# Per-sample sums over partitions in cross-attention: the shares as the stationary operand in four column groups, and a transpose behind them

## The chip, the cores and the metric

The kernel runs on one core of one Trainium2 chip. The metric is the device time of one execution in microseconds (us), the median over runs. Three runs of the kernel before took 1271.40, 1271.95 and 1270.92 us.

## The reference: what is computed

One inference step of a two-layer trunk runs for a prompt of 256 rows and for 8 samples of one row each; both share all weights (model width 1024). Each layer is a half SwiGLU, a mixer (a short convolution in layer 0, a gated recurrence in layer 1), a cross-attention on a memory, and a second half SwiGLU. The part touched here is the samples' cross-attention:

```python
def cross_attn(x, mk, mv, w_q, w_o):
    B, T, D = x.shape
    q = (x @ w_q).reshape(B, T, X_HEADS, X_HEAD_DIM)
    s = jnp.einsum('bthd,bnhd->bhtn', q, mk.astype(q.dtype)).astype(jnp.float32) / math.sqrt(X_HEAD_DIM)
    p = jax.nn.softmax(s, axis=-1).astype(x.dtype)
    o = jnp.einsum('bhtn,bnhd->bthd', p, mv.astype(x.dtype)).reshape(B, T, D)
    return o @ w_o
```

Each of the 8 samples has its own cached keys and values: 256 memory rows, 4 heads of 256 numbers. The prompt projects its own memory with `w_xkv`.

## The kernel before

Activations lie transposed, model width on partitions: eight blocks of 128 partitions by 264 columns (256 prompt columns, then 8 sample columns). Every projection is made three times over split numbers: a value is cut into a high part that the fast matmul format holds exactly and a low rest, and `mm3` (lines 350 to 352) multiplies high by high, high by low and low by high. Weights come as "halves" of 128x1024 through a queue of six raw buffers: SP loads them (L101), ACT rounds them to `wh` (L112), DVE or POOL subtracts to get `wl` (L127). `wh` and `wl` have five buffers each.

TensorE is kept busy by these projections. All else is cut into small generators, and the projection loops call `flow.tick()` after every few matmuls; a tick moves each of three lanes on by one step. A scheduler then sets the final order on each engine, by the program's order and by priorities (`tc.high_priority(offset=HURRY)` lifts a piece). Each engine runs its list strictly in that order.

Cross-attention (`attention`, once per layer) runs in this order: the queries of four heads (`project`), then for each head the prompt's keys and values (`do_kv`, tiles `kv`), then the output projection (`project_late`, tiles `pj` from `oh` and `ol`). In lane 1 run the prompt's scores (`psc`), softmax (`Pp`), transposes (`ppt`, then `PTh` on ACT and `PTl` on DVE) and values (`po`). In lane 0 run the samples' scores and then `sample_rest`.

In `sample_rest` the 2048 memory rows of the 8 samples lie on 128 partitions with 16 rows each (16 partitions belong to one sample). For each of two pairs of heads, DVE adds 16 value rows, weighted by their exponentials, into `acc` (a PSUM bank; L1194 and L1197) and writes the last one into `total` (128 partitions x 2 heads x 256). Every second row ends a step, and two more steps (`LAG`) follow. Then the sum over a sample's 16 partitions is taken by TensorE: `oz` (128x8) holds for a head each partition's share in its sample's column, 0 elsewhere. Line 1214 makes four matmuls per pair, with a 128x128 block of `total` stationary and `oz` moving, so that the result `spt` comes out with width on partitions, 8 columns a block. ACT rounds it into `oh` (L1221), and DVE writes the rest into `ol` (L1222), at the sample columns of this pair's four blocks.

The output projection reads those columns: `until(0)` ahead of its first blocks, and `until(1)` ahead of block 4, which is the second pair's first. So `pj` matmuls on block 4 wait for the second pair's `oh`.

Of the kernel before, what the change touches and what calls it, by code (L numbers as in the profile page):

```python
# [9 lines left out]
F32 = mybir.dt.float32  # L10
# [3 lines left out]
ALU = mybir.AluOpType  # L14
# [3 lines left out]
P = 128  # L18
# [3 lines left out]
NB = 8  # L22
# [5 lines left out]
XD = 256  # L28
RH = 8
NI = NMEM * NB // P  # L30
# [14 lines left out]
STEPS = (3, 5, 7, 9, 11, 13)  # L45
# [210 lines left out]
def trunk_step(ctx: ExitStack, tc: tile.TileContext, ins, consts, outs, stop=None):  # L256
    nc = tc.nc
# [11 lines left out]
    def aux_bank(name):  # L269
        return paux.tile([P, 512], F32, tag="aux", name=name)  # L270

    W = Weights(nc, wp)
    flow = Flow(W)
    ring = Ring(cp)

    ident = cp.tile([P, P], F32, name="ident")
# [31 lines left out]
    def order(ins, first, reason):  # L308
        info = mybir.DependencyInfo(mybir.DependencyClass.NoSync, mybir.DependencyReason.DATA)
        tc.add_manual_dep(ins.ins, first.name, info, reason=reason)  # L310
# [14 lines left out]
    def act(dst, src, func, **kw):  # L325
        in_line(nc.scalar.activation(dst, src, func, **kw))  # L326
# [647 lines left out]
    def attention(l, norm, nxt):  # L974
        with tc.tile_pool(name="at", bufs=1) as ap:
# [4 lines left out]
            for hf, tag in enumerate("hl"):  # L980
                t = ap.tile([P, KT, NC], F32, tag="o" + tag, name=f"spare{hf}", bufs=1)
# [6 lines left out]
            sc = ap.tile([P, XH, NI], F32, name="sc")  # L988
            oz = ap.tile([P, XH, NB], F32, name="oz")
            sampled, ahead = set(), []  # L990
            mx, zs, rz = (ap.tile([P, XH], F32, name=n) for n in ("mxs", "zss", "rzs"))
            tops = ap.tile([P, P], F32, name="tops")
            nc.gpsimd.memset(tops, 0.0)

            def mem_split():
                for _ in range(6):
                    yield
                W.lo = ("p",)
                for k in range(KT):
                    g = gcol("norm_mem", l, k)  # L1000
                    mg = ap.tile([P, NMEM], F32, tag="mg", name=f"mg{k}", bufs=2)
                    W.behind("s", nc.scalar.activation(mg, memT[:, k], AF.Copy, scale=g))
                    nc.scalar.copy(mh[:, k], mg)
                    nc.gpsimd.tensor_sub(ml[:, k], mg, mh[:, k].bitcast(F32))
                    yield
# [144 lines left out]
            def combine():  # L1150

                pt = aux_bank("pst")
                order(nc.tensor.transpose(pt[:XH, :P], mx, ident), flow.passed, "products in line")
                yield
                top, f, g = pt[:XH, 2 * P : 2 * P + NB], pt[:, P + 2 * XH : P + 3 * XH], pt[:, P + 3 * XH : P + 4 * XH]
                nc.vector.tensor_reduce(top, pt[:XH, :P].rearrange("h (b g) -> h b g", b=NB), axis=AX.X, op=ALU.min)
                nc.vector.tensor_copy(tops[:XH].rearrange("h (b g) -> h b g", b=NB), spread(top))
                yield
                order(
                    nc.tensor.matmul(pt[:, P : P + XH], tops, ident[:, :XH], start=True, stop=True),  # L1160
                    flow.passed,
                    "products in line",
                )
# [12 lines left out]
                nc.vector.tensor_mul(g, rz, f)  # L1176
                nc.vector.tensor_mul(
                    oz, g.unsqueeze(2).broadcast_to([P, XH, NB]), own.unsqueeze(1).broadcast_to([P, XH, NB])
                )

            def sample_rest():

                for _ in range(SLACK):
                    yield
                steps = combine()
                for pair in range(XH // 2):
                    acc = aux_bank("acc")
                    total = ap.tile([P, 2, XD], F32, tag="total", name="total", bufs=1)
                    for i in range(NI):
                        t = ring.tiles[l, "v", pair, i // 4].rearrange("p (i h d) -> p i h d", i=4, h=2)  # L1190
                        for j in range(2):
                            p, sums = sc[:, 2 * pair + j, i : i + 1], acc[:, j * XD : j * XD + XD]
                            if i == 0:
                                nc.vector.tensor_scalar(sums, t[:, i % 4, j], p, None, op0=ALU.mult)  # L1194
                            else:
                                dst = total[:, j] if i == NI - 1 else sums
                                nc.vector.scalar_tensor_tensor(  # L1197
                                    dst, t[:, i % 4, j], p, sums, op0=ALU.mult, op1=ALU.add
                                )
                        if i % 4 == 3:  # L1200
                            ring.done((l, "v", pair, i // 4))
                        if pair == 0 and i in STEPS:
                            next(steps, None)
                        if i % 2:
                            yield
                    for _ in range(LAG):
                        yield
                    pt = aux_bank("spt")
                    for j in range(2):
                        for dt in range(2):  # L1210
                            o = pt[:, (2 * j + dt) * NB : (2 * j + dt) * NB + NB]
                            d = slice(dt * P, dt * P + P)
                            order(
                                nc.tensor.matmul(o, total[:, j, d], oz[:, 2 * pair + j], start=True, stop=True),
                                flow.passed,
                                "products in line",
                            )
                    with tc.high_priority(offset=HURRY):
                        ptv = pt[:, : 4 * NB].rearrange("p (t b) -> p t b", b=NB)
                        ohv, olv = (both[tag][:, 4 * pair : 4 * pair + 4, T:] for tag in "hl")  # L1220
                        nc.scalar.copy(ohv, ptv)  # L1221
                        W.after["v"] = nc.vector.tensor_sub(olv, ptv, ohv.bitcast(F32)).ins  # L1222
                    sampled.add(pair)
                    yield

            def until(pair):
                while pair not in sampled:
# [557 lines left out]
```

## Time and profile before

The profiled execution took 1272.46 us; its span, from first to last instruction, is 1270.6 us, so 1.9 us lie around the span. The mean granted TensorE clock is 0.998 of full speed.

| what | value |
|---|---|
| median of three runs | 1271.4 us |
| profiled execution, its span | 1272.46 us, 1270.6 us |
| busy: PE, weight load, DVE, ACT, POOL | 99%, 97%, 66%, 55%, 27% |
| `spt` matmuls (L1214) | 32 records, 3.9 us busy in all |
| pair 1 in layer 0: last row of `total`, first `spt`, first `pj` that needs `oh` | 392.05, 394.60, 395.90 us |

Times in the text are microseconds from the start of the span. A group row gives line, engine, operation, output and inputs, the count, the busy time in us and the mean in ns. A timeline row gives the start, the duration, the engine, the line, the operation, and in brackets the engine's idle time before it with what ended it. One fp32 matmul leaves two records in the trace; matmuls are pipelined, so the distance between starts tells what one costs, and the duration does not.

### The profile page before, as it was taken

What the parts mean: (1) busy time and instruction counts of PE and PEld (TensorE: products, weight loads), DVE (VectorE), ACT (ScalarE), POOL (GpSimd) and SP (SyncE); (2) the same over time, 40 slices, a digit from 0 to 9 for tenths busy, and PEclk for the clock granted to TensorE, in tenths of its full rate; (3) what the DMA queues carried; (4) which work ended last, traced back from release to release, by engine and by line L of the source; (5) the groups of instructions that cost most, each with busy time, mean ns of one, the idle gap of its engine ahead of it and who ended that gap; (6) DMA issues with size and microseconds to landing.
All of it is one profiled execution on the core that took longest, in us unless ns stands there. A gap on an engine that the chain in (4) does not pass through costs nothing.

```text
span 1270.6 us, 25550 instructions
## 1 busy us (share of the span) xinstructions
PE 1257.1 (99%) x10046; PEld 1230.5 (97%) x10046; DVE 841.1 (66%) x1629; ACT 704.4 (55%) x1172; POOL 346.5 (27%) x276
## 2 busy tenths in 40 slices
PE   8999999999999999999999999999999999999997
PEld 8999999999889999999999999999999899999997
DVE  7655467768787655556655535887888787766454
ACT  6455445446665655534645544656576657766543
POOL 2211231223974211132111132000016862112220
PEclk9999999999999999999999999999999999999999
DMA  8795556656999666556666556653638997997551
GB/s 276 246 302 179 166 178 191 195 168 218 313 374 305 184 187 178 180 162 198 190 181 184 173 170 190 190 176 123 192 120 283 352 370 225 286 321 234 166 167 35
DMA packets 269899, 270.97 MB, mean 213 GB/s; under 512 B 8777, under 2 KB 259721, under 8 KB 269266
## 3 DMA queue, kind: packets, MB, share of 16 engines
q1 hardware_dynamic: 264158, 264.50, 66.8%
q10 hardware_dynamic: 5620, 4.83, 1.1%
q8 instruction: 79, 1.29, 0.4%
q14 instruction: 42, 0.34, 0.1%
HBM read 259.19 MB, written 10.10 MB: 212 GB/s over the span
## 4 chain that ended last, share of the span: by engine, by line
PE 90%; DVE 4%; DMA 2%; ACT 2%; issue 1%; POOL 0%; SPq 0%; DVEq 0%; POOLq 0%; ACTq 0%
PE pj L350 20%; PE pj L351 20%; PE pj L352 20%; PE dn L350 7%; PE dn L352 7%; PE dn L351 7%; DMA raw<-in_w_xkv_dram 2%; PE kv L1024 1%; PE kv L1026 1%; PE kv L1025 1%; DVE wl L127 1%; PE pl L1374 1%; DVE xl L376 1%; PE psc L1109 1%; ACT wh L112 1%
## 5 line engine op out<-in xcount | busy, mean ns | idle before, releaser
L127 DVE TENSOR_TENSOR wl<-raw,wh 128x1024 fp32r<-128x1024 f32 (+1 forms) x334 | 411.9, 1238 | 235.6 <-ACT wh L112 223.4
L350 PE MATMUL pj<-xh,wh 128*128 128x264 f32 x1952 | 558.0, 286 | 0.5 <-DVE g L850 0.5
L351 PE MATMUL pj<-xl,wh 128*128 128x264 f32 x1952 | 553.3, 283 | 0.0
L352 PE MATMUL pj<-xh,wl 128*128 128x264 f32 x1952 | 553.1, 283 | 0.0
L112 ACT CAST wh<-raw 128x1024 fp32r<-128x1024 f32 (+1 forms) x406 | 415.4, 1032 | 213.6 <-PE pj L351 114.4
L350 PEld LDWEIGHTS pj<-xh,wh 128*128 128x128 f32 x1952 | 367.6, 188 | 2.3 <-issue 1.4
L351 PEld LDWEIGHTS pj<-xl,wh 128*128 128x128 f32 x1952 | 368.0, 189 | 0.2
L352 PEld LDWEIGHTS pj<-xh,wl 128*128 128x128 f32 x1952 | 366.2, 188 | 0.0
L127 POOL TENSOR_TENSOR wl<-raw,wh 128x1024 fp32r<-128x1024 f32 (+1 forms) x74 | 173.6, 2369 | 126.2 <-ACT wh L112 110.4
L858 POOL TENSOR_TENSOR al<-a,ah 128x264 fp32r<-128x264 f32 x88 | 90.9, 1035 | 411.1 <-ACT ah L857 410.9
L350 PE MATMUL dn<-ah,wh 128*128 128x264 f32 x704 | 200.9, 285 | 0.0
L352 PE MATMUL dn<-ah,wl 128*128 128x264 f32 x704 | 200.0, 284 | 0.0
L351 PE MATMUL dn<-al,wh 128*128 128x264 f32 x704 | 199.4, 283 | 0.0
L352 PEld LDWEIGHTS dn<-ah,wl 128*128 128x128 f32 x704 | 132.7, 188 | 0.0
L350 PEld LDWEIGHTS dn<-ah,wh 128*128 128x128 f32 x704 | 132.4, 188 | 0.2
L351 PEld LDWEIGHTS dn<-al,wh 128*128 128x128 f32 x704 | 132.5, 188 | 0.0
L326 ACT ACTIVATE g<-g 128x264 f32<-128x264 f32 x88 | 36.9, 423 | 76.6 <-DVE g L850 76.6
L857 ACT CAST ah<-a 128x264 fp32r<-128x264 f32 x88 | 36.0, 413 | 68.9 <-DVE a L856 68.8
L371 ACT ACTIVATE xh<-xT,gains 128x264 fp32r<-128x264 f32 x56 | 28.0, 513 | 72.4 <-DVE xT L888 59.2
L389 POOL TENSOR_TENSOR nacc_norm_xattn<-nacc_norm_xattn,nsq 128x264 f32<-128x264 f32 x14 | 12.5, 890 | 174.1 <-ACT nsq L388 173.8
L850 DVE TENSOR_TENSOR g<-pj,R_norm_ffn 128x264 f32<-128x264 f32 x88 | 37.5, 429 | 29.0 <-PE pj L352 28.7
L1197 DVE SCALAR_TENSOR_TENSOR acc<-ring,sc,acc 128x256 f32<-128x256 f32 x112 | 54.5, 486 | 2.5
(357 smaller groups left out, 1560.0 us busy)
## 6 DMA issues: line engine op xcount, KB each, us to landing
raw<-in_w_ffn_gate_dram SPq DMA_DIRECT2D x88, 512.0 KB, 5.7
raw<-in_w_ffn_up_dram SPq DMA_DIRECT2D x88, 512.0 KB, 3.8
raw<-in_w_ffn_down_dram SPq DMA_DIRECT2D x64, 512.0 KB, 3.9
raw<-in_w_xkv_dram SPq DMA_DIRECT2D x64, 256.0 KB, 5.7
ring<-in_cache_mem_v_dram SPq DMA_DIRECT2D x16, 1024.0 KB, 11.5
raw<-in_w_rec_in_dram SPq DMA_DIRECT2D x32, 512.0 KB, 4.3
ring<-in_cache_mem_k_dram SPq DMA_DIRECT2D x12, 1024.0 KB, 7.7
raw<-in_w_ffn_down_dram SPq DMA_DIRECT2D x32, 384.0 KB, 3.1
```

What stands on the lines that cost most here:

```text
L112: ins = self.behind(self.hi[i % len(self.hi)], copy(wh[:, :n], self.raw[i][:, :n]))
L127: ins = eng.tensor_sub(wl[:, :n], self.raw.pop(i)[:, :n], wh[:, :n].bitcast(F32))
L326: in_line(nc.scalar.activation(dst, src, func, **kw))
L350: nc.tensor.matmul(ps, wh[:, s], rh, start=first, stop=False)
L351: nc.tensor.matmul(ps, wh[:, s], rl, start=False, stop=False)
L352: return nc.tensor.matmul(ps, wl[:, s], rh, start=False, stop=last).ins
L371: W.pin(nc.scalar.activation(xh[:, k, :n], src, AF.Copy, scale=gcol(self.name, self.layer, k)))
L376: ins = nc.vector.scalar_tensor_tensor(xl[:, k, :n], src, g, h, op0=ALU.mult, op1=ALU.subtract)
L850: nc.vector.tensor_mul(g, ps, norm.R)
L857: nc.scalar.copy(ah[:, blk], a)
L858: nc.gpsimd.tensor_sub(al[:, blk], a, ah[:, blk].bitcast(F32))
L1197: nc.vector.scalar_tensor_tensor(dst, t[:, i % 4, j], p, sums, op0=ALU.mult, op1=ALU.add)
```

## The change

The four matmuls of a pair change sides. `oz` (8 columns of it) becomes the stationary operand, in one of four column groups of 32 columns, and a 128x128 block of `total` moves. The result is 8 partitions x 128 at partition 0, 32, 64 or 96 of the bank. Four copies bring these strips into a new tile `parts` (zeroed once by POOL), turn by turn on ACT and DVE. In the next step one 128x128 transpose puts them back with width on partitions, and `oh` and `ol` are read from it at a stride of 32 columns.

The first two value rows of the second pair are now issued straight after the first pair's matmuls and copies; the second pair's own loop begins at its third row.

```diff
-                steps = combine()
+                steps, accs, totals = combine(), [], []
+
+                def rows(pair, i):
...
                 for pair in range(XH // 2):
...
+                    for i in range(2 * pair, NI):
+                        rows(pair, i)
                         if i % 2:
                             yield
                     for _ in range(LAG):
                         yield
+                    total = totals[pair]
                     pt = aux_bank("spt")
-                    for j in range(2):
-                        for dt in range(2):
-                            o = pt[:, (2 * j + dt) * NB : (2 * j + dt) * NB + NB]
-                            d = slice(dt * P, dt * P + P)
-                            order(
-                                nc.tensor.matmul(o, total[:, j, d], oz[:, 2 * pair + j], start=True, stop=True),
-                                flow.passed,
-                                "products in line",
-                            )
+                    for c in range(4):
+                        j, dt = divmod(c, 2)
+                        d = slice(dt * P, dt * P + P)
+                        order(
+                            nc.tensor.matmul(
+                                pt[32 * c : 32 * c + NB, :P], oz[:, 2 * pair + j], total[:, j, d], start=True, stop=True
+                            ),
+                            flow.passed,
+                            "products in line",
+                        )
+                    for c in range(4):
+                        at = slice(32 * c, 32 * c + NB)
+                        if c % 2:
+                            nc.vector.tensor_copy(parts[at], pt[at, :P])
+                        else:
+                            nc.scalar.copy(parts[at], pt[at, :P])
+                    if pair == 0:
+                        for i in range(2):
+                            rows(1, i)
+                    yield
+                    po = pt[:, P : 2 * P]
+                    order(nc.tensor.transpose(po, parts, ident), flow.passed, "products in line")
                     with tc.high_priority(offset=HURRY):
-                        ptv = pt[:, : 4 * NB].rearrange("p (t b) -> p t b", b=NB)
+                        ptv = po.rearrange("p (t r) -> p t r", r=32)[:, :, :NB]
                         ohv, olv = (both[tag][:, 4 * pair : 4 * pair + 4, T:] for tag in "hl")
                         nc.scalar.copy(ohv, ptv)
                         W.after["v"] = nc.vector.tensor_sub(olv, ptv, ohv.bitcast(F32)).ins
                     sampled.add(pair)
-                    yield
```

Where the instructions now stand, at the places that the prediction speaks of. First PE in the output projection of layer 0, second pair: before,

```order
L350 MATMUL pj_1_4900<-oh,wh_4805 128x264
L351 MATMUL pj_1_4900<-ol,wh_4805 128x264
L352 MATMUL pj_1_4900<-oh,wl_4820 128x264
L1214 MATMUL spt<-oz,total 128x8 x4
L1123 MATMUL ppt<-ident,Pp 128x128 x4
L350 MATMUL pj_0_4895<-oh,wh_4843 128x264
```

and in the change, where `wh_4818` is the weight tile that the rows above call `wh_4805`:

```order
L1220 MATMUL spt<-total,oz 8x128 x4
L350 MATMUL pj_0_4912<-oh,wh_4818 128x264
L351 MATMUL pj_0_4912<-ol,wh_4818 128x264
...
L351 MATMUL pj_1_4913<-ol,wh_4818 128x264
L352 MATMUL pj_1_4913<-oh,wl_4830 128x264
L1125 MATMUL ppt<-ident,Pp 128x128 x4
L1237 MATMUL spt<-ident,parts 128x128
L350 MATMUL pj_0_4908<-oh,wh_4856 128x264
```

The four products stand twelve `pj` matmuls earlier (ten of the twelve are left out), and the transpose stands where the first `pj` on block 4 follows at once. In layer 1 PE's rows moved in the same way.

Second ACT at the same place in layer 0: before,

```order
L112 CAST wh_5008<-raw_4739 128x1024
L1101 ACTIVATE Pp<-Pp,zsp 128x256 x2
L112 CAST wh_5026<-raw_4791 128x1024
L1221 CAST oh<-spt 128x4x8
L1129 CAST PTh<-ppt 128x512
```

and in the change, with the engines on whose counters a row waits:

```order
L112 CAST wh_5015<-raw_4741 128x1024 [waits DMAHW4_49,PE_49,Pool_49]
L1103 ACTIVATE Pp<-Pp,zsp 128x256 [waits DVE_49]
L1103 ACTIVATE Pp<-Pp,zsp 128x256 [waits Activation_49]
L1231 COPY parts<-spt 8x128 [waits PE_49]
L112 CAST wh_5042<-raw_4800 128x1024 [waits DMAHW5_49,PE_49,Pool_49]
L1231 COPY parts<-spt 8x128 [waits DVE_49]
L1131 CAST PTh<-ppt 128x512 [waits PE_49]
L1241 CAST oh<-spt 128x4x8 [waits PE_49]
```

A weight's rounding now stands between ACT's two copies, and `PTh`, which followed `oh`, stands ahead of it. DVE's two copies each wait for ACT, ACT's second for DVE's first, and the transpose for DVE's second: the four copies go one after the other.

Third ACT in layer 1, where the step that scales the recurrent state (`ring` by `fs`, L326 is the helper's line) shares the place: before,

```order
L1101 ACTIVATE Pp<-Pp,zsp 128x256 x2
L326 ACTIVATE ring_12859<-ring_12859,fs 128x128
L1221 CAST oh<-spt 128x4x8
L112 CAST wh_13072<-raw_12839 128x1024
L1129 CAST PTh<-ppt 128x512
```

and in the change

```order
L1103 ACTIVATE Pp<-Pp,zsp 128x256 x2
L1231 COPY parts<-spt 8x128
L326 ACTIVATE ring_12869<-ring_12869,fs 128x128
L112 CAST wh_13100<-raw_12860 128x1024
L1231 COPY parts<-spt 8x128
L1131 CAST PTh<-ppt 128x512
L326 ACTIVATE ring_12869<-ring_12869,fs 128x128
L1241 CAST oh<-spt 128x4x8
```

Here `oh` stood ahead of the rounding; now a state scaling, the rounding, the second copy, `PTh` and one more state scaling stand between the first copy and it.

Elsewhere little moves. In the first pair, PE has its four products in two twos with one `kv` matmul between them, and the transpose six `kv` matmuls after the first two. DVE's order of the value rows around the second pair's last ones is as before. On SP, one 512 KB weight load of the second SwiGLU stands behind two loads of recurrent state instead of ahead of them, once per layer.

More of the change, by code (lines that the diff above doesn't have):

```diff
@@ L993, in attention @@
             nc.gpsimd.memset(tops, 0.0)
+            parts = ap.tile([P, P], F32, name="parts")
+            nc.gpsimd.memset(parts, 0.0)
             def mem_split():
@@ L1184, in sample_rest @@
                     yield
-                steps = combine()
-                for pair in range(XH // 2):
[L1187 to L1190, printed above, removed]
-                        for j in range(2):
[L1192 to L1198, printed above, removed]
-                                )
[L1200 to L1203, printed above, removed]
+                steps, accs, totals = combine(), [], []
@@ new lines, in rows @@
+                def rows(pair, i):
+                    if i == 0:
+                        accs.append(aux_bank("acc"))
+                    if i == NI - 1:
+                        totals.append(ap.tile([P, 2, XD], F32, tag="total", name="total", bufs=1))
+                    t = ring.tiles[l, "v", pair, i // 4].rearrange("p (i h d) -> p i h d", i=4, h=2)
+                    for j in range(2):
+                        p, sums = sc[:, 2 * pair + j, i : i + 1], accs[pair][:, j * XD : j * XD + XD]
+                        if i == 0:
+                            nc.vector.tensor_scalar(sums, t[:, i % 4, j], p, None, op0=ALU.mult)
+                        else:
+                            dst = totals[pair][:, j] if i == NI - 1 else sums
+                            nc.vector.scalar_tensor_tensor(dst, t[:, i % 4, j], p, sums, op0=ALU.mult, op1=ALU.add)
+                    if i % 4 == 3:
+                        ring.done((l, "v", pair, i // 4))
+                    if pair == 0 and i in STEPS:
+                        next(steps, None)
@@ L1207, in sample_rest @@
                         yield
+                    total = totals[pair]
                     pt = aux_bank("spt")
-                    for j in range(2):
-                        for dt in range(2):
-                            o = pt[:, (2 * j + dt) * NB : (2 * j + dt) * NB + NB]
-                            d = slice(dt * P, dt * P + P)
-                            order(
-                                nc.tensor.matmul(o, total[:, j, d], oz[:, 2 * pair + j], start=True, stop=True),
-                                flow.passed,
-                                "products in line",
-                            )
+                    for c in range(4):
[12 more added lines that the diff above has]
+                            nc.vector.tensor_copy(parts[at], pt[at, :P])
+                        else:
+                            nc.scalar.copy(parts[at], pt[at, :P])
[5 more added lines that the diff above has]
+                    order(nc.tensor.transpose(po, parts, ident), flow.passed, "products in line")
                     with tc.high_priority(offset=HURRY):
-                        ptv = pt[:, : 4 * NB].rearrange("p (t b) -> p t b", b=NB)
+                        ptv = po.rearrange("p (t r) -> p t r", r=32)[:, :, :NB]
                         ohv, olv = (both[tag][:, 4 * pair : 4 * pair + 4, T:] for tag in "hl")
```

## Prediction

> **What bounds the kernel now.** I read the page first.
>
> ```profile
> PE 1257.1 (99%) x10046; PEld 1230.5 (97%) x10046; DVE 841.1 (66%) x1629; ACT 704.4 (55%) x1172; POOL 346.5 (27%) x276
> PEclk9999999999999999999999999999999999999999
> PE 90%; DVE 4%; DMA 2%; ACT 2%; issue 1%; POOL 0%; SPq 0%; DVEq 0%; POOLq 0%; ACTq 0%
> ```
>
> PE is busy almost all the time, at full clock, and the chain that ended last is its own. So an edit is worth what it does to PE: matmul time added or removed, and time in which PE waits. Waits that could swallow a new one are few: between 340 and 400 us, where layer 0's attention runs, the list of waits has one row for PE.
>
> ```profile
> PE po L351 <- DVE PTl L1130: 0.3, 1, 0.3
> ```
>
> The groups by line say what there is to win. All 32 records of the samples' sums load for 4.4 us and multiply for 3.9 us, so the whole of L1214 is about 4 us, 0.3% of the span. (The third row is the nearest transpose, used below.)
>
> ```profile
> L1214 PEld LDWEIGHTS spt<-oz,total 128*128 128x128 f32 x32 | 4.4, 191 | 0.3
> L1214 PE MATMUL spt<-oz,total 128*128 128x8 f32 x32 | 3.9, 240 | 0.0
> L1123 PE MATMUL ppt<-ident,Pp 128*128 128x128 f32 x32 | 5.2, 276 | 0.0
> ```
>
> **Products and transpose on PE.** The timeline around the first pair in layer 0 (layer 1 has the same distances):
>
> ```profile
> 372.09 0.39 PE L1026 MATMUL kv<-wh,ml 128*128 128x512 f32 x1
> 372.32 0.51 PE L1214 MATMUL spt<-oz,total 128*128 128x8 f32 x4
> 372.68 0.68 PE L1109 MATMUL psc<-KTt,qT 128*128 128x256 f32 x2
> 373.19 0.51 PE L1214 MATMUL spt<-oz,total 128*128 128x8 f32 x4
> 373.56 1.54 PE L1109 MATMUL psc<-KTt,qT 128*128 128x256 f32 x6
> 377.72 0.91 ACT L1101 ACTIVATE Pp<-Pp,zsp 128x256 f32<-128x256 f32 x2
> 379.05 0.60 PE L1123 MATMUL ppt<-ident,Pp 128*128 128x128 f32 x4
> ```
>
> From start to next start the two halves of `spt` take 0.36 and 0.37: 0.73 us removed. For what comes in there is a near row, since the recurrence already multiplies narrow stationaries in four column groups against 128 columns:
>
> ```profile
> 837.96 0.28 PE L352 MATMUL pj<-xh,wl 128*128 128x264 f32 x1
> 838.17 1.93 PE L1459 MATMUL pqs<-ring,qfz 128*4 128x128 f32 x64
> 840.03 0.39 PE L350 MATMUL pj<-xh,wh 128*128 128x264 f32 x1
> 840.26 0.28 PE L351 MATMUL pj<-xl,wh 128*128 128x264 f32 x1
> ```
>
> 64 records between 838.17 and 840.03 are 0.029 us each. A `pj` matmul elsewhere starts 0.12 after the last (394.36 to 394.48, below); here the one before takes 0.21 and the one after 0.23, so going in and out costs 0.20 together. The change has eight records per pair. In the first pair they come in two fours, each with two of the four groups, between 0.029 (as here) and 0.058 a record (only two strips side by side): 0.12 to 0.23, plus 0.20. Two of them are 0.64 to 0.86. The transpose is one of the kind of `ppt`, of which four take 0.49 (395.41 to 395.90, below), so 0.12, or up to 0.20 if it pays an entry of its own like the groups. That is 0.76 to 1.06 for 0.73. I take **+0.1 us per layer**, near the lower end since PE's rows overlap wherever they can, and keep 0 and +0.3.
>
> On the entry cost the Trainium skill has a rule that speaks against this change: TensorEngine Tiling (Array Packing), section Key Properties, says that a change of tiling mode, as against a change of tile, drains TensorE. The 0.20 above agrees with it. Without such a drain the first pair would cost 0.4 less.
>
> The first pair's copies are hidden: behind the products stand the `psc` (1.54) and five `kv` of 0.23 (372.09 to 372.32), 2.7 us, before the transpose. One thing comes nearer. `oh` now stands between ACT's two exponentials, so `Pp` ends later than its 378.63 (377.72 + 0.91) by up to 0.4 by my estimate (0.18 for `oh`, the rest a wait for the transpose), and PE arrives at `ppt` 0.1 later; the 0.42 of slack are used up. That is the upper end above.
>
> **The second pair, layer 0.** Here `oh` is wanted at once. The timeline of PE, ACT and DVE:
>
> ```profile
> 392.05 0.87 DVE L1197 SCALAR_TENSOR_TENSOR total<-ring,sc,acc 128x256 f32<-128x256 f32 x2
> 393.07 0.17 DVE L1099 RECIPROCAL zsp<-zsp 128x2 f32<-128x2 f32 x1
> 393.87 0.91 ACT L1101 ACTIVATE Pp<-Pp,zsp 128x256 f32<-128x256 f32 x2
> 394.36 0.29 PE L351 MATMUL pj<-ol,wh 128*128 128x264 f32 x1
> 394.48 0.28 PE L352 MATMUL pj<-oh,wl 128*128 128x264 f32 x1
> 394.60 0.95 PE L1214 MATMUL spt<-oz,total 128*128 128x8 f32 x8
> 394.72 1.05 ACT L112 CAST wh<-raw 128x1024 fp32r<-128x1024 f32 x1
> 395.41 0.64 PE L1123 MATMUL ppt<-ident,Pp 128*128 128x128 f32 x4
> 395.67 0.18 ACT L1221 CAST oh<-spt 128x32 fp32r<-128x32 f32 x1
> 395.90 0.63 PE L350 MATMUL pj<-oh,wh 128*128 128x264 f32 x3
> 396.08 0.59 ACT L1129 CAST PTh<-ppt 128x512 fp32r<-128x512 f32 x1 [0.23 <-PE ppt L1123]
> 397.95 0.68 DVE L1130 TENSOR_TENSOR PTl<-ppt,PTh 128x512 fp32r<-128x512 f32 x1
> ```
>
> Before, PE does not wait: `oh` ends at 395.85, `pj` starts at 395.90, just when `ppt` is through. The new order gives this, step by step.
>
> - PE comes to the products twelve `pj` sooner, 394.60 - 12 x 0.12 = 393.15. `total` is ready at 392.05 + 0.87 = 392.92, so no wait, with 0.2 to spare. Products are out at about 393.6.
> - ACT is in line behind both `Pp`, which wait for `zsp`. Its first copy starts where the rounding did, at 394.72. For a copy of 128 columns I go between rows: ACT takes 0.18 for 32 and 0.59 for 512, so 0.26; DVE takes 0.68 for 512 and 0.19 for 32 (`ol` at 1049.31, below), so 0.29.
> - The rounding next in ACT's line writes a buffer whose last reader is the `pj` at 394.36 (over at 394.65). The products now stand ahead of it, eight records and an entry, 0.43, so it is freed at about 395.1. Rounding takes 1.05, and the next may start 0.1 before it ends.
> - ACT's second copy, 396.05 to 396.3. DVE's second, to 396.6. The transpose at 396.65. PE, which saves nothing on the products till here, is at that point at 394.60 + 0.43 + 0.49 = 395.5: **it waits 1.1 us.**
> - The transpose's result takes 0.27, the mean of the same tile size in `ppt` (276 ns). `PTh` holds ACT from 396.2 to 396.8, `oh` goes 396.95 to 397.15, and `pj` starts at 397.2: **a second wait of 0.4.**
>
> Against 395.90 that is **+1.3 us**; the PE time saved here (0.81 by 0.43 + 0.12) is in it. `PTl`, ahead of `ol` on DVE, then ends at about 397.6, before PE has got through four `pj` and one `po`, so at most 0.1 more. What is late next costs nothing: the `wl` behind `ol` starts 1.8 later, but PE with it.
>
> **The second pair, layer 1.** The same place, with state scalings on ACT:
>
> ```profile
> 1047.37 0.91 ACT L1101 ACTIVATE Pp<-Pp,zsp 128x256 f32<-128x256 f32 x2
> 1048.10 0.95 PE L1214 MATMUL spt<-oz,total 128*128 128x8 f32 x8
> 1048.18 0.39 ACT L326 ACTIVATE ring<-ring,fs 128x128 f32<-128x128 f32 x1
> 1048.91 0.64 PE L1123 MATMUL ppt<-ident,Pp 128*128 128x128 f32 x4
> 1049.31 0.19 DVE L1222 TENSOR_TENSOR ol<-spt,oh 128x32 fp32r<-128x32 f32 x1 [2.58 <-ACT oh L1221]
> 1049.33 0.39 PE L350 MATMUL pj<-oh,wh 128*128 128x264 f32 x1
> ```
>
> ACT's first copy goes 1048.18 to 1048.43, the scaling to 1048.7, the rounding to 1049.75, the second copy to 1049.9, DVE to 1050.2, the transpose from 1050.25 to 1050.5. `PTh` ends at 1050.4, the second scaling at 1050.7, `oh` at 1050.85, and `pj` starts at 1050.9 instead of 1049.33: **+1.55 us**, of which 1.25 ahead of the transpose.
>
> **The rest.** The value rows that move sooner start in DVE's gap in the first pair, and the last ones still stand behind the second pair's maximum of the scores, which PE's `psc` gates; they neither win nor lose. Two zeroings on POOL (27% busy) are hidden behind the whole attention. On SP a weight load slips behind two state loads:
>
> ```profile
> 391.21 0.79 SPq L101 DMA_DIRECT2D raw<-in_w_ffn_gate_dram  x1
> 392.39 7.18 SPq L820 DMA_DIRECT2D ring<-in_state_rec_dram  x4
> 409.27 1.05 ACT L112 CAST wh<-raw 128x1024 fp32r<-128x1024 f32 x1 [0.27 <-PE pj L351]
> ```
>
> Half of the four loads' 7.18 puts it at about 395 instead of 391; it is rounded at 409.27, and there ACT waits for PE. Ten microseconds of cover; were they gone, it would cost what the load is late, up to 3.6.
>
> **The sum.** 0.1 + 1.3 for layer 0 and 0.1 + 1.55 for layer 1 are +3.05 us. The profiled execution's 1272.46 would become 1275.5. It lies 1.1 above the median of the three runs, so the median goes from 1271.4 to **1274.5 us**, 0.24% more. About 0.2%, 2.5 us, is what a measurement of this kernel can tell from no change.
>
> The ends: with copies of 0.2, the rounding not kept back by PE and quick hand-overs each layer's wait is 0.4 shorter and the first pair costs nothing, +2.0. With 0.15 more at each of the four hand-overs and the first pair's 0.3, it is +4.3.
>
> **The rivals.**
>
> *Smaller than can be told, 1272.5 to 1273.8 us.* The same chain, at its lower end: the rounding starts right after the first copy instead of waiting for PE, and the copies and hand-overs are shorter than between the rows. For it: of the +3.05 only 0.55 are over the bound, 0.07 on each of eight copies and hand-overs. Against: each end is bounded by the 1.05 of a rounding that ACT cannot pass.
>
> *Not slower, 1269.7 us.* The groups pack fully, and the strips are back before PE needs them. Then a layer's two pairs cost 16 x 0.029 + 2 x 0.12 = 0.70 instead of 0.73 + 0.81 = 1.54, 0.84 less, 1.7 less in both. It decides at one point: `oh` has to be written when PE ends `ppt`, at 395.5. For it: the products start 1.45 sooner. Against: ACT's second copy stands behind a rounding that cannot end before 395.8 even if it starts at 394.72. The Trainium skill is for it, in TensorEngine Tiling (Array Packing), section When to Use Tiling: with a free dimension of 32 or less on the moving side it advises to swap the sides and use four column tiles. It prices the products alone; by it 0.84 a layer would be won, and no row of this order bears that out.
>
> *Worse, 1276.3 us.* The first pair's `ppt` too waits, since `oh` stands between the two exponentials: 0.4 per layer there, the first pair at its upper end (0.2 more), and 0.3 in each second pair for `ol` behind `PTl`, 0.9 a layer on top of the forecast, +4.9. For it: 0.42 of slack only. Against: `psc` and with it `Pp`'s inputs are late by what PE is late.
>
> **How the numbers follow.** Forecast (slower by 2.5 to 4.3) 0.58, smaller 0.29, not slower 0.06, worse 0.07. Faster by over 0.2% would need 2.5 us, more than the 1.7 of the best case: 0.03, the rest of that case counts as the same. Slower: 0.58 + 0.07 = 0.65. Same: 0.29 + 0.03 = 0.32. The range leaves out the not-slower case, the lowest part of the smaller one and the end of the worse: 1271.9 to 1276.2.
>
> **What would show it.** In the list of waits for PE, a new row of about 1.1 us in each layer at the transpose, released by DVE's copy into `parts`, and one of 0.3 to 0.5 at the first `pj` after it, released by ACT's `oh`. In ACT's timeline a rounding of 1.05 between two copies of about 0.26. The products' eight records within 0.45. Wrong would be: `pj` on block 4 following the transpose with no idle time, a gap over 0.3 at the first pair's `ppt`, or the difference of the spans lying outside the stretches 372 to 400 and 1025 to 1053.

## The result and the profile after

The changed kernel takes 1274.55 us, the median of nine runs (1274.34 to 1276.27), against 1271.18 us of the kernel before in the same session (nine runs, 1270.76 to 1271.95). The ratio is 1.003, with a 95% interval of 1.0022 to 1.0038: slower by 3.4 us. The forecast was 1274.5. The profiled execution took 1275.11 us, its span 1273.3 us at a granted clock of 0.998, as before.

The engines' busy times on the page of the changed kernel have hardly moved; PE has 0.5 us more than before.

```profile
PE 1257.6 (99%) x10050; PEld 1228.2 (96%) x10050; DVE 841.7 (66%) x1637; ACT 706.8 (56%) x1180; POOL 347.0 (27%) x278
```

What is new stands in PE's list of waits (what waited, released by what; us in total, times, the longest). The first two rows were not there before; the third was there twice as often over the whole run, which matters further down.

```profile
PE spt L1237 <- DVE parts L1229: 2.5, 2, 1.2
PE pj L350 <- ACT oh L1241: 0.6, 2, 0.3
PE po L351 <- DVE PTl L1132: 0.3, 1, 0.3
```

The second pair in layer 0, from the timeline of the changed kernel (start, duration, engine and line, in brackets the engine's idle time and its releaser):

```profile
393.17 0.28 PE L352 MATMUL pj<-oh,wl 128*128 128x264 f32 x1
393.38 0.41 PE L1220 MATMUL spt<-total,oz 128*8 128x128 f32 x8
393.71 0.39 PE L350 MATMUL pj<-oh,wh 128*128 128x264 f32 x1
393.94 0.28 PE L351 MATMUL pj<-ol,wh 128*128 128x264 f32 x1
394.81 0.24 ACT L1231 COPY parts<-spt 8x128 f32<-8x128 f32 x1
395.27 0.60 PE L1125 MATMUL ppt<-ident,Pp 128*128 128x128 f32 x4
395.39 1.05 ACT L112 CAST wh<-raw 128x1024 fp32r<-128x1024 f32 x1 [0.34 <-issue]
396.46 0.26 ACT L1231 COPY parts<-spt 8x128 f32<-8x128 f32 x1
396.75 0.30 DVE L1229 COPY parts<-spt 8x128 f32<-8x128 f32 x1 [1.38 <-ACT parts L1231]
397.11 0.33 PE L1237 MATMUL spt<-ident,parts 128*128 128x128 f32 x1 [1.23 <-DVE parts L1229]
397.47 0.19 ACT L1241 CAST oh<-spt 128x32 fp32r<-128x32 f32 x1
397.71 0.76 PE L350 MATMUL pj<-oh,wh 128*128 128x264 f32 x4 [0.28 <-ACT oh L1241]
```

A rounding of 1.05 us stands between ACT's two copies, and DVE's last copy waits 1.38 for ACT's second. PE waits for that copy and then for `oh`. In layer 1 the same two waits read:

```profile
1051.40 0.33 PE L1237 MATMUL spt<-ident,parts 128*128 128x128 f32 x1 [1.23 <-DVE parts L1229]
1052.06 0.75 PE L350 MATMUL pj<-oh,wh 128*128 128x264 f32 x4 [0.33 <-ACT oh L1241]
```

In the first pair nothing waits, but the products stand in two fours with a `kv` between them:

```profile
371.97 0.39 PE L1028 MATMUL kv<-wh,ml 128*128 128x512 f32 x1
372.29 0.39 PE L1220 MATMUL spt<-total,oz 128*8 128x128 f32 x4
372.61 0.49 PE L1026 MATMUL kv<-wh,mh 128*128 128x512 f32 x1
373.03 0.39 PE L1220 MATMUL spt<-total,oz 128*8 128x128 f32 x4
373.36 1.99 PE L1111 MATMUL psc<-KTt,qT 128*128 128x256 f32 x8
```

**Two stretches.** A time of 1272 us scatters by more than most of what follows, so each kernel was also read by two stretches of PE's timeline. The *first* runs from the first `kv` behind the second head's values to the first `pj` on `oh` and holds the first pair; the *second* runs from there to the last `pj` on `oh` and holds the second pair. Both hold the same matmuls in every kernel, apart from those for the samples' sums. Their ends in layer 0 of the kernel before:

```profile
367.75 0.39 PE L1024 MATMUL kv<-wh,mh 128*128 128x512 f32 x1
383.66 0.28 PE L350 MATMUL pj<-oh,wh 128*128 128x264 f32 x1
411.99 0.28 PE L352 MATMUL pj<-oh,wl 128*128 128x264 f32 x1
```

and of the changed kernel:

```profile
367.62 0.39 PE L1026 MATMUL kv<-wh,mh 128*128 128x512 f32 x1
383.80 0.28 PE L350 MATMUL pj<-oh,wh 128*128 128x264 f32 x1
413.78 0.28 PE L352 MATMUL pj<-oh,wl 128*128 128x264 f32 x1
```

That is 15.91 and 28.33 us before, 16.18 and 29.98 after. In the table, all kernels of this study: the stretches as differences from 15.91 and 28.33 (these hold for both layers of the kernel before), layer 0 and layer 1, their sum, and the difference of the median times on the same chip with the ratio's interval.

| kernel | first stretch | second stretch | sum | median minus before | ratio, interval |
|---|---|---|---|---|---|
| the change | +0.27, +0.27 | +1.65, +1.73 | +3.92 | 1274.55 - 1271.18 = +3.37 | 1.0022 to 1.0038 |
| rows only | +0.05, +0.05 | -0.02, -0.02 | +0.06 | 1271.21 - 1271.31 = -0.10 | 0.9992 to 1.0010 |
| products only | +0.30, +0.30 | +1.33, +1.65 | +3.58 | 1274.10 - 1271.31 = +2.79 | 1.0015 to 1.0033 |
| copies on DVE | +0.26, +0.26 | +1.02, +1.02 | +2.56 | 1273.23 - 1271.31 = +1.92 | 1.0006 to 1.0024 |
| rounding after the copies | +0.26, +0.27 | +1.00, +1.24 | +2.77 | 1273.64 - 1271.31 = +2.33 | 1.0009 to 1.0027 |
| copies on DVE, rounding after `oh` | +0.26, +0.27 | +0.73, +0.67 | +1.93 | 1273.07 - 1271.14 = +1.93 | 1.0007 to 1.0025 |
| copies in turn, rounding after `oh` | +0.26, +0.26 | +0.73, +1.16 | +2.41 | 1273.86 - 1271.14 = +2.72 | 1.0012 to 1.0031 |
| groups added to before | +0.46, +0.45 | +0.36, +0.36 | +1.63 | 1272.89 - 1271.14 = +1.75 | 1.0006 to 1.0024 |
| first pair only | +0.26, +0.26 | -0.10, -0.10 | +0.32 | 1271.00 - 1271.14 = -0.14 | 0.9990 to 1.0008 |
| groups together, copies on DVE, rounding after `oh` | -0.13, -0.12 | +0.80, +0.80 | +1.35 | 1272.50 - 1271.09 = +1.41 | 1.0001 to 1.0019 |
| first pair only, groups together | +0.04, +0.03 | -0.03, -0.05 | -0.01 | 1270.76 - 1271.09 = -0.33 | 0.9988 to 1.0006 |

The two columns agree within 0.8 us; where they part most, the medians are the smaller ones.

### The profile page after: what moved, and what is told of

It is laid out like the page before. It is cut to its first block, busy times and chain, and to the rows that moved or that the text cites. A ratio compares the mean times of both kernels' runs of the same rounds, so it can differ in the third digit from the quotient of the medians.

```text
span 1273.3 us, 25575 instructions
## 1 busy us (share of the span) xinstructions
PE 1257.6 (99%) x10050; PEld 1228.2 (96%) x10050; DVE 841.7 (66%) x1637; ACT 706.8 (56%) x1180; POOL 347.0 (27%) x278
## 4 chain that ended last, share of the span: by engine, by line
PE 92%; DVE 3%; DMA 2%; ACT 2%; issue 1%; POOL 0%; SPq 0%; DVEq 0%; ACTq 0%; POOLq 0%
PE pj L350 20%; PE pj L351 20%; PE pj L352 19%; PE dn L350 7%; PE dn L352 7%; PE dn L351 7%; PE kv L1026 2%; PE kv L1028 2%; PE kv L1027 2%; PE pl L1393 1%; DVE wl L127 1%; PE pj L445 1%; DMA raw<-in_w_xkv_dram 1%; PE psc L1111 1%; DVE xl L376 1%
## 5 line engine op out<-in xcount | busy, mean ns | idle before, releaser
L326 ACT ACTIVATE g<-g 128x264 f32<-128x264 f32 x88 | 36.9, 424 | 76.9 <-DVE g L850 76.9
```

## The experiments

The theory at the start: the second pair loses by a chain through ACT, in which a weight rounding stands ahead of what the result needs, and PE's own time changes little. Rivals: the value rows that begin two steps sooner cost the time; the alternation of ACT and DVE costs it, whatever stands between; the column groups themselves cost it.

### Which half of the change

Rows only: the kernel before, with the first two value rows of the second pair issued as in the change.

```diff
-                    for i in range(NI):
+                    for i in range(2 * pair, NI):
+                        rows(pair, i)
...
+                    if pair == 0:
+                        for i in range(2):
+                            rows(1, i)
```

> Only the earlier value rows: the second pair's first two rows stand behind the first pair's products, and the products and their rounding stay as before, without strips, copies and transpose. Theory A (the loss is PE's wait for the four copies, of which one stands behind a weight's rounding on ACT): no such chain here, so within 0.6 us of the kernel before, 1270.6 to 1271.8, and no wait over 0.3 us at the products or at the first matmul that reads their result. Rival B (the earlier rows crowd DVE or the score path and cost the time): 1273 or more. The order of the work puts the samples' result ahead of the softmax's scaling on ACT, which may hold that up by 0.3 to 0.6 us per layer; if PE feels it, up to 1272.2.

It took 1271.21 us, 0.10 below the kernel before; in the attention PE has no wait at all for the samples' sums, and the stretches are within 0.05. The moved rows neither win nor lose.

Products only: the change without the early rows (`for i in range(NI)`, nothing issued behind the first pair).

> Only the products' new form, with strips, copies and transpose, and the value rows as before. Theory A: the loss stays, since the result still hangs on ACT behind a rounding of 1.05 us. The scheduler puts the prompt's values ahead of the transpose here, so the wait should move: PE waits some 1.2 us per layer for the prompt's weights (PTh, PTl), which stand behind the rounding on ACT, and less than 0.3 at the transpose. Sum 0.25 per layer in the first pair and about 1.2 in the second: 1273.3 to 1274.6. Rival B (the earlier rows cost the time): back near 1271.2. Rival C (four column groups and the transpose cost the time on PE itself): 1274.5 with no wait on other engines.

It took 1274.10 us, +2.79. The early rows are thus not needed for a loss. It shows in another place, though. In this order `ppt` comes ahead of the products, and the prompt's values ahead of `oh`; from the timeline of layer 0:

```profile
394.30 0.78 PE L1125 MATMUL ppt<-ident,Pp 128*128 128x128 f32 x4
394.42 1.05 ACT L112 CAST wh<-raw 128x1024 fp32r<-128x1024 f32 x1
395.37 0.58 ACT L1131 CAST PTh<-ppt 128x512 fp32r<-128x512 f32 x1
395.98 0.69 DVE L1132 TENSOR_TENSOR PTl<-ppt,PTh 128x512 fp32r<-128x512 f32 x1 [3.05 <-ACT PTh L1131]
396.73 0.39 PE L350 MATMUL po<-PTh,Vh 128*128 128x256 f32 x1 [1.31 <-DVE PTl L1132]
```

The copies are hidden behind the twelve `po`, and PE waits for `PTl` instead (1.31 here, 1.6 in layer 1). The expectation named this place and its size, but for a reason that holds only in part. `ppt` ends at 395.08 and `PTh` starts at 395.37, so the rounding holds it up by at most 0.29. The rest is `PTh` (0.58) and `PTl` (0.69) themselves, for which PE has only the eight records as cover in this order. This run says that the new form loses without the early rows; it does not show what a rounding costs.

### ACT's order

All four strips copied by DVE:

```diff
-                        if c % 2:
-                            nc.vector.tensor_copy(parts[at], pt[at, :P])
-                        else:
-                            nc.scalar.copy(parts[at], pt[at, :P])
+                        nc.vector.tensor_copy(parts[at], pt[at, :P])
```

> The change with all four copies on DVE instead of turn by turn on ACT and DVE. Theory A: DVE is free there (it idled 1.7 and 1.4 us around its copies), four copies of 0.29 are out by about 395.2 in layer 0, and the wait of 1.23 us per layer at the transpose is gone. What stays is the result's rounding behind the weight's rounding on ACT: a wait of 0.3 to 0.6 per layer at the first matmul that reads it, and 0.25 per layer in the first pair. 1271.9 to 1272.8. Rival C (the groups and the transpose cost PE the time): stays at 1274 to 1275.

It took 1273.23 us, +1.92: higher than the 1271.9 to 1272.8 expected of the theory. The wait at the transpose is gone, but the rounding now stands ahead of `oh` (timeline, layer 0):

```profile
395.31 1.05 ACT L112 CAST wh<-raw 128x1024 fp32r<-128x1024 f32 x1 [0.98 <-issue]
395.52 0.28 PE L1234 MATMUL spt<-ident,parts 128*128 128x128 f32 x1
396.27 0.18 ACT L1238 CAST oh<-spt 128x32 fp32r<-128x32 f32 x1
396.50 0.64 PE L350 MATMUL pj<-oh,wh 128*128 128x264 f32 x3 [0.58 <-ACT oh L1238]
```

The transpose is through at 395.80 and `oh` starts at 396.27, when the rounding lets ACT go. The other part of the excess is that the scheduler now put the eight records in two fours, with `pj` between, as in the rows of the later run with the copies on DVE, below.

The copies in turn as in the change, but the rounding held back until ACT's second copy:

```diff
-                            nc.scalar.copy(parts[at], pt[at, :P])
+                            W.after["s"] = nc.scalar.copy(parts[at], pt[at, :P]).ins
```

> The change with one order more: weights are rounded on ACT only after its second copy, so both copies stand side by side and the rounding behind them. Theory A: ACT's copies at 394.8 and 395.4, DVE's second out at about 396.0, the transpose waits 0.2 to 0.4 instead of 1.23 us per layer. But now the rounding stands between the copies and the result's own rounding, so the first matmul that reads it waits 0.4 to 0.6 per layer. Together 1272.2 to 1273.3. Rival D (the hand-overs between ACT and DVE as such cost the time, whatever stands between them): the wait at the transpose stays over 0.9, 1274 or more.

It took 1273.64 us, +2.33, slightly above the expectation. PE's waits, both layers:

```profile
PE pj L350 <- ACT oh L1241: 1.2, 2, 0.6
PE spt L1237 <- DVE parts L1229: 0.6, 2, 0.4
```

The wait at the transpose fell from 2.5 to 0.6 in all, so most of it was the rounding and not the alternation. The rounding moved one place down and doubled the wait for `oh`, from 0.6 to 1.2.

So it was held back further, behind `oh`, once with all copies on DVE and once with copies in turn:

```diff
+                    W.held = pair == 1
                     yield
+                    W.held = False
...
-                        nc.scalar.copy(ohv, ptv)
+                        into = nc.scalar.copy(ohv, ptv)
+                        if pair:
+                            W.after["s"] = into.ins
```

> All four strips are copied by DVE, and the second pair's rounding of a weight tile is put behind oh in ACT's line. If the loss of the second pair is ACT's order (the rounding of 1.05 us standing ahead of something that the result needs), the stretch from the first to the last pj on oh, 29.98 and 30.06 us in the changed kernel and 28.33 in the kernel before, comes to 28.5 to 28.9, with no wait of PE at the transpose and at most 0.5 at the first pj. The first pair keeps its 0.27 per layer, so the whole is 1271.9 to 1272.8 us, 0.6 to 1.5 above the kernel before. If instead the columns' form itself costs PE time (four strips, the change of tiling, the transpose), the stretch stays at 29.2 or more although PE has nothing to wait for, and the time is 1273.2 or more.

> The changed kernel's copies on ACT and DVE in turn, with the second pair's rounding put behind oh in ACT's line. If the rounding between ACT's two copies and the one ahead of oh make the waits, the wait at the transpose falls from 1.2 to 0.3 or less, that at the first pj to 0.3 or less, the stretch from the first to the last pj on oh to 28.7 to 29.1, and the time is 1272.2 to 1273.0 us. If the alternation of ACT and DVE alone makes them (each copy waiting for the one before), the wait at the transpose stays over 0.6 and the time over 1273.2.

With the copies on DVE it took 1273.07 us and the second stretch 29.06 and 29.00: between what the two theories expected, so both have a part. The timeline of layer 0 shows them apart:

```profile
392.61 0.28 PE L351 MATMUL pj<-ol,wh 128*128 128x264 f32 x1
392.82 0.39 PE L1220 MATMUL spt<-total,oz 128*8 128x128 f32 x4
393.14 0.39 PE L352 MATMUL pj<-oh,wl 128*128 128x264 f32 x1
393.37 0.28 PE L350 MATMUL pj<-oh,wh 128*128 128x264 f32 x1
393.58 0.39 PE L1220 MATMUL spt<-total,oz 128*8 128x128 f32 x4
393.90 0.39 PE L351 MATMUL pj<-ol,wh 128*128 128x264 f32 x1
395.43 0.27 PE L1125 MATMUL ppt<-ident,Pp 128*128 128x128 f32 x1
395.62 0.18 ACT L1240 CAST oh<-spt 128x32 fp32r<-128x32 f32 x1 [1.52 <-PE spt L1236]
395.71 1.05 ACT L112 CAST wh<-raw 128x1024 fp32r<-128x1024 f32 x1
395.86 0.63 PE L350 MATMUL pj<-oh,wh 128*128 128x264 f32 x3 [0.17 <-ACT oh L1240]
```

The rounding is behind `oh`, and from the last `ppt` to `pj` PE loses 0.43 - 0.12 = 0.31. The rest is PE's own: each four takes 0.32 to the next start, and the `pj` ahead of and behind each take 0.20 more together than the usual 0.12.

With the copies in turn it took 1273.86 us, more than the 1272.2 to 1273.0 expected. The two waits in all:

```profile
PE pj L350 <- ACT oh L1243: 0.7, 2, 0.5
PE spt L1239 <- DVE parts L1229: 0.6, 2, 0.4
```

In layer 0 they are 0.3 and 0.2, as expected; in layer 1 0.5 and 0.4, because the state scalings on ACT took the rounding's place between the copies. The alternation alone is thus worth about 0.3 at the transpose in layer 0, not 1.2.

### What the column groups cost by themselves

The kernel before with four such products added per pair, read by nobody:

```diff
+                    for c in range(4):
+                        j, dt = divmod(c, 2)
+                        d = slice(dt * P, dt * P + P)
+                        order(nc.tensor.matmul(
+                            pt[32 * c : 32 * c + NB, P : 2 * P], oz[:, 2 * pair + j], total[:, j, d], start=True, stop=True
+                        ), flow.passed, "products in line")
```

> The kernel before with four products in column groups added in each pair (eight records); nobody reads their results, so there is nothing to wait for, only PE's own time. If the groups cost what the recurrence's rows gave (0.23 for eight and 0.20 for going in and out), the first pair's stretch (from the first kv after the second head's values to the first pj on oh, 15.91 us before) grows by 0.4 and the second pair's (28.33) by 0.4, 1.7 us in all. If a change of tiling costs more than the recurrence's rows showed, each grows by 0.55 or more, 2.2 us or more in all; the changed kernel's second pair points there, with eight records in 0.53.

It took 1272.89 us, +1.75, and the stretches grew by 0.46, 0.45, 0.36 and 0.36: the first theory's 0.4 each. The first pair's timeline:

```profile
372.78 0.51 PE L1214 MATMUL spt<-oz,total 128*128 128x8 f32 x4
373.22 0.41 PE L1222 MATMUL spt<-total,oz 128*8 128x128 f32 x8
373.56 1.56 PE L1109 MATMUL psc<-KTt,qT 128*128 128x256 f32 x6
```

Eight records take 0.34 from start to next start, and the four old ones ahead of them 0.44 instead of 0.37. A four in the run with the copies on DVE took 0.32. Call a *stay* the records in column groups that stand side by side on PE, with no other matmul between. Between four records and eight the price of a stay hardly changes.

The new form in the first pair alone:

```diff
-                    for c in range(4):
+                    if pair == 0:
+                        for c in range(4):
...
+                    else:
+                        for j in range(2):
+                            for dt in range(2):
```

> The new form in the first pair alone; the second pair is computed as before. If the two pairs cost what their stretches say, the first stretch is 16.18 (0.27 longer), the second 28.33, there is no wait of PE for the samples' sums, and the time is 0.5 us above the kernel before, too little for its interval to exclude zero. If the second pair's loss were partly the first pair's (what is late there pushing ACT's roundings), the second stretch is longer than 28.5 too, and the whole 1 us or more above.

It took 1271.00 us, 0.14 below the kernel before, where 0.5 above it was expected; the stretches' sum is +0.32. The first stretch is 16.17, the second 28.23, without a wait. The pairs' costs are separate: what the first pair does late pushes nothing in the second.

Then the eight records of a pair were kept together, by putting each product in line behind the one before it, in the order 2, 3, 0, 1, so that the first already needs the second head's `total`. Once with all copies on DVE and the rounding after `oh`, once in the first pair alone:

```diff
-                    for c in range(4):
+                    before = flow.passed
+                    for c in (2, 3, 0, 1):
...
+                        order(prod, before, "products in line")
+                        before = prod.ins
```

> As the run with all copies on DVE and the rounding behind oh, but a layer's eight records of each pair stand together on PE, where they were two fours with other matmuls between. If a stay in column groups costs nearly the same for four records as for eight (0.32 against 0.34 from start to next start, and 0.20 around it), the first pair's stretch falls from 16.17 to 15.65 to 15.8, below the 15.91 of the kernel before, and in the second pair PE's own part falls by 0.5; there the products now start two matmuls later and the transpose stands behind ppt, so PE waits 0.4 to 0.9 for oh, and its stretch is 28.6 to 29.1. The whole is 1271.3 to 1272.3 us. If instead each record costs its share, the first stretch stays at 16.0 or more and the whole at 1272.3 or more.

> The new form in the first pair alone, with its eight records together. If the 0.27 us per layer come from going into the groups twice, the first stretch falls to 15.65 to 15.8 plus whatever PE waits at the transpose, which now stands four kv behind the products (0 to 0.5); the second stretch is 28.23 as in the run without this. The whole is then 0.3 to 0.7 below the kernel before, 1270.4 to 1270.9 us, which its interval cannot tell from no change. If the 0.27 have another cause, the first stretch stays at 16.1 or more and the time at that of the kernel before.

In both pairs it took 1272.50 us, +1.41; the first stretch fell from 16.17 to 15.78, as the theory expected, below the kernel before:

```profile
372.16 0.41 PE L1220 MATMUL spt<-total,oz 128*8 128x128 f32 x8
372.50 1.99 PE L1111 MATMUL psc<-KTt,qT 128*128 128x256 f32 x8
```

One stay of 0.34 has replaced two of 0.32 and 0.33. In the second pair the products came two matmuls later and the transpose behind `ppt`, so PE waits again for `oh` (0.4 in each layer), and the second stretch, 29.13, is just above the 28.6 to 29.1 expected; so is the whole, by 0.2.

In the first pair alone it took 1270.76 us, 0.33 below the kernel before; the interval of 0.9988 to 1.0006 does not tell that from no change. Its first stretch is 15.95. The eight records again take 0.34; of the 0.17 against the run with both pairs, 0.12 stand ahead of `ppt`. No kernel here is measurably faster than the one before.

### The second pair of layer 0, put together

A stay of eight costs 0.33 + 0.20, the transpose 0.12, and 0.81 is saved: PE's own part is -0.16. With two stays of four it is 2 x (0.32 + 0.20) + 0.12 - 0.81 = +0.35. The waits are taken from start to next start, less what the matmul takes without a wait (0.49 for four `ppt` as in the kernel before, 0.12 for one transpose or `ppt`); in the changed kernel that is 397.11 - 395.27 - 0.49 = 1.35 and 397.71 - 397.11 - 0.12 = 0.48.

| kernel | PE's own | ahead of the transpose | ahead of the first `pj` | sum | stretch |
|---|---|---|---|---|---|
| the change | -0.16 | 1.35 | 0.48 | +1.67 | +1.65 |
| rounding after the copies | -0.16 | 0.28 | 0.83 | +0.95 | +1.00 |
| copies in turn, rounding after `oh` | -0.16 | 0.28 | 0.48 | +0.60 | +0.73 |
| copies on DVE | +0.35 | 0 | 0.74 | +1.09 | +1.02 |
| copies on DVE, rounding after `oh` | +0.35 | 0 | 0.31 | +0.66 | +0.73 |
| groups together, copies on DVE, rounding after `oh` | -0.16 | 0.18 | 0.57 | +0.59 | +0.80 |

The sums meet the stretches within 0.13, in the last row within 0.21. Moving the rounding behind `oh` takes 0.92 of the 1.65 away (29.98 to 29.06 with copies in turn); what is left is the chain itself, four strips, a transpose and `oh` one after another, and in the second pair it did not fit into the cover in any order tried.

## Why the prediction was right, point by point

**The place and the mechanism held.** The list of waits has the two rows that were named, at the transpose 1.2 (predicted 1.1 and 1.25) and at `pj` 0.3 (0.3 to 0.5). ACT's timeline has the rounding between two copies of 0.24 and 0.26 (0.26), DVE's copies take 0.28 to 0.30 (0.29). The eight records take 0.33 (at most 0.45), going in and out 0.21 + 0.23 - 2 x 0.12 = 0.20 (0.20), and the transpose, where it does not wait (copies on DVE), 0.12. That holding back the rounding takes away most of the wait at the transpose shows that it was the cause. The moved rows cost nothing, as the run with them alone shows.

**The first pair was mis-sized:** +0.27 per layer where +0.1 was taken, near the upper end of 0 and +0.3. The term is the price of a four, "between 0.029 (as here) and 0.058 a record", 0.12 to 0.23; it takes 0.32 and 0.33. The recurrence's 64 records in a row were the wrong row to divide: at four or eight records the runs show a price per stay, hardly one per record. The trace shows where it lies: of the second pair's eight records the last starts 0.13 behind the first, and the next matmul starts 0.20 behind the last; the same 0.20 stand behind the 64 records, which themselves start within 1.66 us. With the eight together the stretch is 0.13 shorter than before instead of 0.27 longer.

With 0.65 for the two fours the prediction's other terms would give 0.65 + 0.40 + 0.12 - 0.73 = +0.44. What kept the sum near is a term that it put at nothing: the old form had a price around it too. In the kernel before, the `psc` behind each two of the old products takes 0.299 to the next start, the one after it 0.216, so 2 x 0.083 = 0.17 per pair went with the old form. That the two errors had opposite signs was luck.

The rule of the Trainium skill, TensorEngine Tiling (Array Packing), section Key Properties, that a change of mode drains TensorE, agrees with the 0.20 around each stay, paid twice in the two fours and once where the eight stand together. That it is a drain is not shown, and about half of the 0.20 is no mark of the groups: in the kernel before, the first `pj` behind the plain transposes `ppt` also takes 0.23 to the next start (395.90 to 396.13).

**The second pair was 0.35 too low in layer 0** (+1.65 for +1.3) and 0.18 in layer 1 (+1.73 for +1.55). From the products to the transpose it took 397.11 - 393.38 = 3.73 where 3.50 was worked out. The rounding began 0.06 later against the products than reckoned; "the next may start 0.1 before it ends" was wrong for the copy, which started at 396.46, 0.02 behind the rounding's end (395.39 + 1.05); the last 0.05 are in the hand-overs to DVE and to PE. And PE saves 0.16 on the products and the transpose, not 0.26: the 0.43 taken for eight records (0.23 and the 0.20 around them) is 0.33 and 0.20.

**The sum of +3.05 met +3.37 by the medians**; by the stretches it is +3.92. That the forecast time came out within 0.1 of the measured one, nearer than its parts, is luck: the kernel before is 0.2 lower in the longer series (1271.18), and PE wins back time outside the stretches. "The difference of the spans lying outside the stretches" was named as a sign of error, and part of it does: the spans differ by 2.7. The last section says where the profiled executions differ outside. The upper end is not what its terms give: 0.15 at four hand-overs in each layer and 0.2 more for each first pair are +1.6, so +4.65 and not +4.3.

**The rivals.** *Smaller than can be told* did not come: its quick hand-overs were not there, and the rounding began 0.34 behind the end of the first copy, not right after it. *Not slower*: the groups do pack, and with the eight together PE's own part is below nothing, -0.13 in the first pair and -0.16 in the second of a layer. The -0.84 for both left out the 0.20 around each stay, which the prediction itself had read, and took 0.23 for the 0.33 of eight records. In the second pair the strips were back in time in two runs with the copies on DVE, but `oh` never was. So the advice of the Trainium skill, TensorEngine Tiling (Array Packing), section When to Use Tiling, to swap the sides holds for the products, with a third of the 0.84 that was worked out from rows. The section names no price, and the hand-overs outweigh it. *Worse*: the first pair's `ppt` did not wait in the changed kernel; in the last run of the study 0.12 stand ahead of it, so the slack was indeed used up.

## What to carry to other kernels

When a matmul's sides are swapped to save PE time, price the way back of the result as a chain on the engines that carry it, with what already stands in their lines: one rounding of 1.05 us cost more than the whole work saved. A stay in column groups has a price per stay (here 0.33 and 0.20 around it, for four records or eight), so keep its matmuls together. Moving the obstacle one place down the line carried a third of the wait with it (1.07 less ahead of the transpose, 0.35 more ahead of `pj`); only behind the last thing that the bound engine needs does it cost nothing there.

## What was not expected of the hardware

The landing of one weight load differs from run to run of like programs. In the kernel before, ACT waits for it in both layers:

```profile
348.43 1.05 ACT L112 CAST wh<-raw 128x1024 fp32r<-128x1024 f32 x1 [1.99 <-DMA raw<-in_w_xkv_dram]
1001.95 1.05 ACT L112 CAST wh<-raw 128x1024 fp32r<-128x1024 f32 x1 [1.99 <-DMA raw<-in_w_xkv_dram]
```

and in the changed kernel only in layer 0:

```profile
348.30 1.05 ACT L112 CAST wh<-raw 128x1024 fp32r<-128x1024 f32 x1 [2.14 <-DMA raw<-in_w_xkv_dram]
```

In the profiles of the other runs the wait is between nothing and 1.59, apart from 2.00 in layer 1 of the run with groups added. Where it is about 2 us, and only there, PE waits 0.3 at the second `po` of that head; this is gone in layer 1 of the changed kernel, and its delay against the kernel before falls there from 1.3 to 0.7. PE also enters the first stretch of layer 0 sooner by 0.13 (367.62 against 367.75) and wins 0.5 at 418 us, at the `ps_ms` behind the attention, where its delay falls from 1.8 to 1.3. Together this is why the spans differ by 2.7 and the stretches by 3.9. Whether the landing also makes the scatter of the times is not shown; no run changed the load.

Copies of different strips took turns: ACT's second began when DVE's first was over and the other way round. The rows show a wait of one on the other each time, and these waits stand in the program, as its order ahead of the prediction shows; whether the chip could read the strips at once was not tried. The Trainium skill, TensorEngine Tiling (Array Packing), section PSUM Bottleneck, warns that the way back out of PSUM may become the bound and advises to use both ScalarE and VectorE for it; the warning fits the waits here. The advice brought next to nothing: the four copies take 1.17 us from first start to last end with both engines in turn and 1.19 with DVE alone (both with the rounding behind `oh`). With the eight records together PE loses 0.28 ahead of the transpose in the first case and 0.18 in the second.
